# A hybrid decoder layer: the sums of the second head's attention weights on GpSimd

## The chip, the cores and the metric

One core of a Trainium2 chip runs the whole kernel. The metric is device time in microseconds, lower is better. Engines are named as the profile names them: PE is TensorE (PEld its weight loads), DVE is VectorE, ACT is ScalarE, POOL is GpSimd, SP is SyncE, which issues the DMAs.

## The reference

One layer over 2048 frames and 16 learned meta tokens, width 1024. A normalised input goes through one combined projection; its columns feed three mixers: forgetting attention (8 heads of 64), gated linear attention, and a gated linear recurrence. Their gated outputs go through an output projection, a second norm and the residual addition. What matters here is the forgetting attention:

```python
s = jnp.einsum('bhqd,bhkd->bhqk', qi, kf) * scale + cqi[..., None] - c[:, :, None, :]
mask = (kpos[None, :] <= qpos[:, None]) & valid[None, :]
p = jax.nn.softmax(jnp.where(mask, s, NEG), axis=-1)
return jnp.einsum('bhqk,bhkd->bhqd', p, vf)
```

The softmax needs, for each query, the sum of its weights over all keys. It is that sum which the change moves.

## The kernel before, in words

`hybrid_kernel` makes a list of jobs, each with a part that prepares (projections) and a part that mixes. While job i mixes, job i + 1 prepares: `merge` takes turns between the two in a fixed ratio, so the order of the instructions on each engine is fixed by the program. Jobs come in this order: the gated linear attention, the recurrence, then the 16 attention jobs, for each pair of heads p (0 to 3) and each chunk c of 512 queries (0 to 3). After them comes the output projection. A third stream, `wout_ready`, runs beside the attention jobs: it scales the output weights and splits them into halves (L1476 on DVE takes the remainder of a half, L1409 differences of blocks).

`fox_attend` (L1276) does one attention job with its two heads h = 0 and 1. It goes over 4c + 5 blocks of keys, j = 0, 1, and so on; a block has 128 keys, the last one 16. For each block:

- PE makes the logits of both heads in one pair of PSUM banks (`sq`, L1297, and on the diagonal a mask, L1303). From j = 4c on, `off` leaves out the queries that lie before the block, so that the width of a head is 512 at j = 4c, then 400, 272, 144 and, with 16 keys, 16.
- ACT takes the exponential of both heads into `pt` (L1305). There are three `pt` buffers, so the exponential of j + 3 needs everything that reads the `pt` of j to be done.
- The weights are added up over blocks in `za[0]` and `za[1]`, one for each head, with a row for each key of a block and a column for each query. At j = 1 DVE adds blocks 0 and 1 (L1310). From j = 2 on line 1313 adds block j to `za[h]`. Head 0 is always added on DVE. Head 1 is added on POOL at even j and on DVE at odd j.
- PE multiplies `pt` by the values (`fv`, L1325), two blocks behind.

At the end ACT copies the result (L1331), POOL multiplies it by the gate (L1332), and PE adds up the rows of `za` with a matrix of ones (L1336). The sums then go through DRAM to be spread and inverted. The rest of that is left for the next attention as two late functions: behind its add of j = 1 DVE takes the reciprocal, and behind its add of j = 2 POOL multiplies the result by it (L1351), for which it waits for the DMA of `rz`.

Beside the blocks of an attention runs `fox_prepare` of the next: projections (L485, L497), and for each 128 queries and each chunk of keys a product `mq` (L1231, L1235) whose maximum DVE takes straight from PSUM (`mj`, L1239). `mq` has one pair of banks, so the next product waits until DVE has read the last.

The framework puts in the waits: an engine runs its instructions in program order, and each waits for the writers and readers of its tiles.

Of the kernel before, what the change touches and what calls it, by code (L numbers as in the profile page):

```python
# [28 lines left out]
NCH = SEQ // CH  # L29
# [71 lines left out]
def unit(k, tag, shape, dt=F32, name=None):  # L101
    wide = tag in ("AT", "QA", "QB", "KA", "KB", "WC", "OO", "OX", "T", "Z", "ZZ", "WH", "WL")
    n = 1
    for d in shape[1:]:
        n *= d
    full = k.wk.tile([P, 2 * CH if wide else CH], dt, name=name or tag, tag=tag, bufs=BUFS[tag])
    ap = full[0:shape[0], 0:n]
    if len(shape) == 3:
        ap = ap.rearrange("p (a b) -> p a b", b=shape[2])
    return ap  # L110
# [5 lines left out]
def bank(k, tag="pj"):  # L116

    return k.ps.tile([P, CH], F32, name=tag, bufs=PBUFS[tag])


def pair(k, tag):

    return k.ps.tile([P, 2, CH], F32, name=tag, bufs=1)
# [44 lines left out]
def hybrid_kernel(tc, xT, x, w_grp, w_fa, vecs, w_a2, w_r, w_i, w_out, post_g, masks, out, yD=None):  # L168
    nc = tc.nc
    with ExitStack() as es:  # L170
# [56 lines left out]
        for p in range(4):  # L227
            for c in range(NCH):
                load = fox_loads(p + 1) if p < 3 else {}
                jobs.append((load.get(c, []), fox_prepare(k, p, c), fox_attend(k, p, c), 4 * c + 5,  # L230
                             FILL[c] if (p, c) != (3, 3) else LAST_FILL))
# [269 lines left out]
def rows_spread(k, i, ps):  # L501

    nc = k.nc
    D = k.rowD[i]
    zs = unit(k, "ZS", [P, CH], name="zs")
    nc.scalar.copy(out=zs, in_=ps)
    for h in range(2):
        nc.sync.dma_start(out=D[0, h:h + 1, :], in_=zs[64 * h:64 * h + 1, :])
    zt = small(k, "zt", [P, 8], bufs=2)
    nc.sync.dma_start(out=zt, in_=D[0].rearrange("h (q e) -> (h q) e", e=8))  # L510
    return D, zt


def rows_back(k, D, zt):
    k.nc.sync.dma_start(out=D[1].rearrange("h (q e) -> (h q) e", e=8), in_=zt)
# [754 lines left out]
def end_late(k):  # L1270
    for f in k.late:
        f(nullcontext())
    k.late = []


def fox_attend(k, p, c):  # L1276
    nc, st = k.nc, k.st
    qh, ql, qx = st.pop(("q", p, c))
    gate = st.pop(("gate", p, c))
    K = st["k", p]  # L1280
    pv = bank(k, "fv")
    za = [unit(k, "ZA", [P, CH], name="za") for _ in range(2)]
    nj = 4 * c + 5
    todo = []
    for j in range(nj):

        V = K.V[j // 4]
        d = j - 4 * c
        off = 0 if d <= 0 else P * d - NM
        m = NM if d == 4 else P  # L1290
        kk = slice(P * (j % 4), P * (j % 4) + m)
        sp = pair(k, "sq")
        pt = k.wk.tile([P, 2, CH], F32, name="pt", tag="PT", bufs=3)
        for i, (a, b) in enumerate(((K.hi, qh), (K.hi, ql), (K.lo, qh), (K.x, qx))):
            for h in range(2):
                hs = slice(64 * h, 64 * h + 64)
                nc.tensor.matmul(out=sp[0:m, h, off:], lhsT=a[j // 4][hs, kk], rhs=b[hs, off:], start=i == 0,  # L1297
                                 stop=i == 3 and d < 0)
        if d >= 0:
            v0 = NM if d == 0 else 0  # L1300
            v1 = NM if d == 4 else P
            for h in range(2):
                nc.tensor.matmul(out=sp[0:m, h, off:off + v1 - v0], lhsT=k.identb[0:m, 0:m],  # L1303
                                 rhs=k.trib[0:m, v0:v1], start=False, stop=True)
        k.exp = nc.scalar.activation(pt[0:m, :, off:], sp[0:m, :, off:], AF.Exp, scale=K.esc[0:m]).ins  # L1305
        for h in range(2):
            if j == 1:
                if off:
                    nc.vector.tensor_copy(za[h][:, 0:off], p0[:, h, 0:off])
                add = nc.vector.tensor_tensor(za[h][:, off:], p0[:, h, off:], pt[:, h, off:], op=ALU.add).ins  # L1310
            elif j > 1:
                eng = nc.gpsimd if h == 1 and j % 2 == 0 else nc.vector
                add = eng.tensor_tensor(out=za[h][0:m, off:], in0=za[h][0:m, off:], in1=pt[0:m, h, off:],  # L1313
                                        op=ALU.add).ins

        if 1 <= j <= 2 and k.late:
            k.late.pop(0)(k.tc.issue_after(add))
        if j == 0:
            p0 = pt
        todo.append((j, m, off, pt, V))  # L1320
        if len(todo) == 3 or j == nj - 1:
            for j1, m1, off1, pt1, V1 in todo[:1] if j < nj - 1 else todo:
                for h in range(2):
                    hs = slice(64 * h, 64 * h + 64)
                    nc.tensor.matmul(out=pv[hs, off1:], lhsT=V1[0:m1, j1 % 4, hs], rhs=pt1[0:m1, h, off1:],  # L1325
                                     start=j1 == 0, stop=j1 == nj - 1)
            todo = todo[1:]
        yield

    o = unit(k, "R", [P, CH], name="fo")  # L1330
    nc.scalar.copy(out=o, in_=pv)  # L1331
    nc.gpsimd.tensor_tensor(o, o, gate, op=ALU.mult)  # L1332
    zp = bank(k, "fx")
    for h in range(2):
        hs = slice(64 * h, 64 * h + 64)
        nc.tensor.matmul(out=zp[hs, :], lhsT=k.ones[:, 0:64], rhs=za[h], start=True, stop=True)  # L1336
    D, zt = rows_spread(k, NCH * p + c, zp)
    inv = k.w["fg", p][3]

    def rows(behind):  # L1340
        with behind:
            nc.vector.reciprocal(zt, zt)
        nc.vector.tensor_scalar(out=zt, in0=zt, scalar1=inv, scalar2=None, op0=ALU.mult)
        rows_back(k, D, zt)

    def scaled(behind):
        rz = unit(k, "RS", [P, CH], name="rz")
        for h in range(2):
            nc.sync.dma_start(out=rz[64 * h:64 * h + 64, :], in_=D[1, h:h + 1, :].to_broadcast([64, CH]))
        with behind:  # L1350
            nc.gpsimd.tensor_tensor(o, o, rz, op=ALU.mult)  # L1351
        k.store = k.mark = nc.sync.dma_start(out=k.yD[P * p:P * p + P, CH * c:CH * c + CH], in_=o).ins

    k.late = [rows, scaled]
    if (p, c) == (3, NCH - 1):
        end_late(k)
# [318 lines left out]
```

## Time and profile before

| | |
|---|---|
| median of 3 runs | 1989.29 us (1987.2 to 1992.66) |
| the profiled execution | 1977.47 us |
| its span, first to last instruction | 1975.8 us |
| PE busy | 1880.4 us (95%) |
| DVE busy | 1268.3 us (64%) |
| ACT busy | 1012.7 us (51%) |
| POOL busy | 565.4 us (29%) |
| adds of line 1313 on DVE | 208 |
| adds of line 1313 on POOL | 80 |

The profile is of one execution; its span is the time from the first to the last instruction. An engine is busy while it runs an instruction; waiting and issuing DMAs are not counted. The attention jobs lie between about 900 and 1676 us. In a timeline row the bracket at the end gives the idle time of the engine before the instruction and what ended it.

### The profile page before, as it was taken

The page shows a single profiled execution, that of the slowest core. Times are in us where ns is not written, and L with a number is a line of the kernel's source. Part 1 is how long each engine was busy: PE and PEld are TensorE (multiplying, and loading weights), DVE is VectorE, ACT ScalarE, POOL GpSimd, SP SyncE. Part 2 cuts the span into 40 slices and gives each one's busy share as a digit, 9 for nine tenths or more (in the row PEclk, how much of TensorE's full clock was granted, in tenths as well). Part 3 has the DMA queues.
Part 4 walks back from the last instruction along what each step waited for, and adds up shares of the span by engine and source line. Part 5 has one row for each costly group of instructions (what it writes and reads, how often), then busy time and mean ns, then how long its engine had stood idle before and what let it go on. Part 6 is the DMA issues. An engine that isn't in the chain of part 4 may idle for free. (4 is left out here: it accounts for less than half of the span.)

```text
span 1975.8 us, 39430 instructions
## 1 busy us (share of the span) xinstructions
PE 1880.4 (95%) x15988; PEld 976.2 (49%) x15988; DVE 1268.3 (64%) x2850; ACT 1012.7 (51%) x1561; POOL 565.4 (29%) x548
## 2 busy tenths in 40 slices
PE   6888999999999999999999999999999987999997
PEld 5555666666555555555434443444344422444443
DVE  6766454454787788673665368747874665667674
ACT  7755642344888887762345234523442335444441
POOL 3443133221434333320122111211221124433422
PEclk9999999999999999999999999999999988999999
DMA  6200121211211100121132113412431128723411
GB/s 225 76 8 29 43 86 29 75 55 30 82 52 45 44 22 22 43 74 44 61 101 69 30 46 118 128 45 65 118 97 44 44 59 294 234 87 122 134 43 64
DMA packets 116135, 152.69 MB, mean 77 GB/s; under 512 B 18793, under 2 KB 75817, under 8 KB 115953
## 3 DMA queue, kind: packets, MB, share of 16 engines
q1 hardware_dynamic: 115952, 150.18, 24.0%
q8 instruction: 125, 2.05, 0.4%
q14 instruction: 58, 0.47, 0.1%
HBM read 108.71 MB, written 41.33 MB: 76 GB/s over the span
## 5 line engine op out<-in xcount | busy, mean ns | idle before, releaser
L485 PE MATMUL pj<-xhl,whl 128*128 128x512 f16 (+3 forms) x3960 | 813.1, 356 | 16.1 <-ACT whl L437 7.4
L485 PEld LDWEIGHTS <-whl 128*128 128x128 f16 x3984 | 364.8, 98 | 405.1 <-issue 80.7
L1305 ACT ACTIVATE pt<-sq,consts 128x1024 f32<-128x1024 f32 (+4 forms) x176 | 163.4, 929 | 252.5 <-PE sq L1303 97.7
L1313 POOL TENSOR_TENSOR za<-za,pt 128x512 f32<-128x512 f32 (+1 forms) x80 | 99.0, 1238 | 535.4 <-ACT pt L1305 489.1
L1239 DVE CUSTOM_DVE_ANT_0 mj<-mq,CB 128x512 bf16<-128x512 f32 (+4 forms) x344 | 189.9, 579 | 56.7 <-PE mq L1231 28.5
L1604 PEld LDWEIGHTS <-whl 128*128 128x128 f16 x1344 | 130.6, 98 | 160.6 <-issue 4.4
L497 PEld LDWEIGHTS <-xhl 128*128 128x128 f16 (+1 forms) x3264 | 184.9, 97 | 31.6 <-issue 27.3
L497 PE MATMUL pj<-whl,xhl 128*128 128x128 f16 (+1 forms) x3024 | 189.6, 219 | 0.0
L1313 DVE TENSOR_TENSOR za<-za,pt 128x512 f32<-128x512 f32 (+3 forms) x208 | 121.3, 606 | 84.6 <-ACT pt L1305 81.2
L1325 PE MATMUL fv<-pt,fv 128*64 128x512 f32 (+4 forms) x688 | 171.3, 538 | 0.0
L1604 PE MATMUL pj<-xhl,whl 128*128 128x512 f16 x768 | 168.6, 380 | 0.0
L1297 PE MATMUL sq<-QA,KA 64*128 64x512 f16 (+4 forms) x1032 | 127.0, 341 | 9.5 <-ACT pt L1305 9.5
L1604 PE MATMUL pj<-ts,whl 128*128 128x512 f16 x576 | 125.7, 379 | 0.0
L563 DVE SCALAR_TENSOR_TENSOR xc<-lx,consts,xc 128x448 f32<-128x448 f32 (+1 forms) x120 | 93.4, 778 | 3.6
L1588 POOL TENSOR_TENSOR o<-o,xt 128x512 f32<-128x512 f32 x31 | 51.6, 1684 | 120.3 <-issue 91.7
L1570 ACT ACTIVATE sqo<-o 128x512 bf16<-128x512 f32 x32 | 20.1, 630 | 127.7 <-DVE o L1564 127.7
L521 ACT ACTIVATE gate<-pj,consts 128x512 f32<-128x512 f32 (+2 forms) x72 | 46.1, 641 | 72.4 <-PE pj L485 59.4
L1297 PEld LDWEIGHTS <-KA 64*128 64x128 f16 (+1 forms) x1032 | 40.3, 94 | 82.5 <-issue 59.9
L1610 DVE SCALAR_TENSOR_TENSOR o<-pj,consts,o 128x512 f32<-128x512 f32 x56 | 41.1, 745 | 61.1 <-PE pj L1604 56.9
L598 POOL TENSOR_TENSOR v<-a 128x448 f32<-128x448 f32 (+1 forms) x40 | 38.4, 961 | 129.5 <-ACT a L596 115.4
L1231 PE MATMUL mq<-KA,QA 64*128 64x512 f16 (+4 forms) x344 | 60.8, 342 | 10.6 <-DVE consts L1239 9.0
L522 DVE SCALAR_TENSOR_TENSOR gate<-gate,pj 128x512 f32<-128x512 f32 (+2 forms) x72 | 45.1, 627 | 39.4 <-ACT gate L521 38.1
(263 smaller groups left out, 2786.4 us busy)
## 6 DMA issues: line engine op xcount, KB each, us to landing
wr<-in_w_out_dram SPq DMA_DIRECT2D x64, 256.0 KB
y<-yD SPq DMA_DIRECT2D x32, 512.0 KB
raw<-in_w_grp_dram SPq DMA_DIRECT2D x28, 512.0 KB
wD<-ws SPq DMA_DIRECT2D x56, 256.0 KB
CB<-c32D SPq DMA_DIRECT2D x32, 256.0 KB
rawf<-in_w_grp_dram SPq DMA_DIRECT2D x16, 512.0 KB
xhl<-wD SPq DMA_DIRECT2D x16, 512.0 KB
xt<-in_x_dram SPq DMA_DIRECT2D x16, 512.0 KB
```

The lines of the kernel that those rows point to most:

```text
L485: nc.tensor.matmul(out=ps, lhsT=a[:, kt, 0:m], rhs=b[:, kt, u0:u0 + n], start=i == 0, stop=i == 23)
L497: nc.tensor.matmul(out=ps, lhsT=a[:, kt, u0:u0 + m], rhs=b[:, kt, :], start=i == 0, stop=i == 23)
L521: k.act = nc.scalar.activation(out, ps, AF.Tanh, scale=hinv).ins
L563: nc.vector.scalar_tensor_tensor(out=xc, in0=lx[:, j:j + n], scalar=cw(j), in1=xc, op0=ALU.mult, op1=ALU.add)
L1231: nc.tensor.matmul(out=ps[h][:, 0:n], lhsT=qh[hs, P * i:P * i + P], rhs=d.hi[pc][hs, 0:n], start=True, stop=pc < c)
L1239: nc.vector.tensor_tensor_reduce(out=junk[:, h, 0:n], in0=ps[h][:, 0:n], in1=d.cb[pc][:, h, 0:n], scale=1.0, scalar=-3e38, op0=ALU.add, op ...
L1297: nc.tensor.matmul(out=sp[0:m, h, off:], lhsT=a[j // 4][hs, kk], rhs=b[hs, off:], start=i == 0, stop=i == 3 and d < 0)
L1305: k.exp = nc.scalar.activation(pt[0:m, :, off:], sp[0:m, :, off:], AF.Exp, scale=K.esc[0:m]).ins
L1313: add = eng.tensor_tensor(out=za[h][0:m, off:], in0=za[h][0:m, off:], in1=pt[0:m, h, off:], op=ALU.add).ins
L1325: nc.tensor.matmul(out=pv[hs, off1:], lhsT=V1[0:m1, j1 % 4, hs], rhs=pt1[0:m1, h, off1:], start=j1 == 0, stop=j1 == nj - 1)
L1588: eng.tensor_tensor(out=o, in0=o, in1=xt[:, h, :], op=ALU.add)
L1604: nc.tensor.matmul(out=ps, lhsT=a[:, kt, :], rhs=w[b + kt // 4][:, :, kt % 4, :], start=kt + j == 0, stop=(kt, j) == (KT - 1, 2))
```

## The change

One line of `fox_attend` chooses the engine of the adds from j = 2 on. Before, POOL has the even blocks of head 1. After, POOL has all blocks of head 1 from j = 2 on, except in the last attention (p = 3, c = 3), where it has the even ones as before. Head 0 stays on DVE.

```diff
             elif j > 1:
-                eng = nc.gpsimd if h == 1 and j % 2 == 0 else nc.vector
+                eng = nc.gpsimd if h == 1 and (j % 2 == 0 or (p, c) != (3, NCH - 1)) else nc.vector
                 add = eng.tensor_tensor(out=za[h][0:m, off:], in0=za[h][0:m, off:], in1=pt[0:m, h, off:],
                                         op=ALU.add).ins
```

## Rows read from the trace of the kernel before

**Rows 1.** The page, part 1: busy time of each engine.

```profile
PE 1880.4 (95%) x15988; PEld 976.2 (49%) x15988; DVE 1268.3 (64%) x2850; ACT 1012.7 (51%) x1561; POOL 565.4 (29%) x548
```

**Rows 2.** The chain that ended last: start us, us, what.

```profile
1655.85 0.02 issue
...
1678.24 18.06 PE pj L1604 x81
```

**Rows 3.** Windows: busy time by stretch.

```profile
core 0: us, PE busy (x) PEld busy (x) DVE busy (x) ACT busy (x) POOL busy (x), PEclk, DMA share, GB/s
900.00:1600.00 700.00, 682.29 (x5111) 292.02 (x5109) 447.63 (x1264) 275.99 (x410) 129.08 (x105) 1.00 0.23 71
1180.00:1220.00 40.00, 38.18 (x246) 12.57 (x245) 36.23 (x89) 18.89 (x24) 8.96 (x8) 1.00 0.37 120
1380.00:1420.00 40.00, 37.52 (x234) 11.85 (x232) 35.81 (x87) 18.61 (x23) 10.08 (x8) 1.00 0.34 97
1425.00:1435.00 10.00, 8.51 (x45) 3.58 (x43) 5.93 (x27) 5.10 (x7) 0.00 (x0) 0.92 0.31 87
1435.00:1445.00 10.00, 10.00 (x54) 2.42 (x53) 9.11 (x16) 4.82 (x6) 1.34 (x1) 0.91 0.50 140
```

**Rows 4.** Waits of PE from 900 to 1600 us: total, times, longest.

```profile
PE mq L1231 <- DVE consts L1239: 8.3, 12, 1.5
PE sq L1297 <- ACT pt L1305: 3.5, 5, 2.0
```

**Rows 5.** Groups of DVE by form, 900 to 1680 us: busy us, mean ns, idle before.

```profile
L1313 DVE TENSOR_TENSOR za<-za,pt 128x512 f32<-128x512 f32 x120 | 85.1, 732 | 47.3 <-ACT pt L1305 44.1 <-POOL za L1313 2.8
...
L1476 DVE SCALAR_TENSOR_TENSOR ws<-wt,consts,ws 128x512 f16<-128x512 f32 x32 | 29.6, 926 | 6.6 <-ACT ws L1475 6.6
...
L1313 DVE TENSOR_TENSOR za<-za,pt 128x400 f32<-128x400 f32 x24 | 15.1, 658 | 10.2 <-ACT pt L1305 10.2
...
L1313 DVE TENSOR_TENSOR za<-za,pt 128x144 f32<-128x144 f32 x32 | 9.6, 336 | 16.7 <-ACT pt L1305 16.7
```

**Rows 6.** Groups of POOL by form, 900 to 1680 us.

```profile
L1313 POOL TENSOR_TENSOR za<-za,pt 128x512 f32<-128x512 f32 x48 | 79.3, 1653 | 344.6 <-ACT pt L1305 327.3 <-DVE za L1313 9.9 <-DVE consts L1239 4.6
...
L1313 POOL TENSOR_TENSOR za<-za,pt 128x272 f32<-128x272 f32 x16 | 15.9, 994 | 133.7 <-ACT pt L1305 121.0 <-DVE consts L1239 11.6 <-DVE za L1313 1.1
```

**Rows 7.** Timeline of p 1, c 3: start us, us, engine, instruction, idle before.

```profile
1274.17 0.69 DVE L1313 TENSOR_TENSOR za<-za,pt 128x512 f32<-128x512 f32 x1 [0.36 <-ACT pt L1305]
...
1274.22 1.77 POOL L1313 TENSOR_TENSOR za<-za,pt 128x512 f32<-128x512 f32 x1 [5.55 <-ACT pt L1305]
...
1274.79 1.76 DVE L1476 SCALAR_TENSOR_TENSOR ws<-wr,consts,ws 128x512 f16<-128x512 f32 x1
```

**Rows 8.** Timeline of p 2, c 2, j 7: two adds, then PE's wait.

```profile
1402.02 0.74 DVE L1476 SCALAR_TENSOR_TENSOR ws<-wr,consts,ws 128x512 f16<-128x512 f32 x1
...
1403.40 1.28 DVE L1313 TENSOR_TENSOR za<-za,pt 128x512 f32<-128x512 f32 x2
...
1404.83 1.27 POOL L1313 TENSOR_TENSOR za<-za,pt 128x512 f32<-128x512 f32 x1 [4.49 <-DVE za L1313]
...
1405.96 0.39 PE L1231 MATMUL mq<-KA,QA 64*128 64x512 f16 x2 [1.50 <-DVE consts L1239]
```

**Rows 9.** Timeline of p 3, c 2, j 2 and 3: L1476 beside POOL's add.

```profile
1587.53 1.16 DVE L1476 SCALAR_TENSOR_TENSOR ws<-wt,consts,ws 128x512 f16<-128x512 f32 x1
...
1589.35 0.39 PE L1231 MATMUL mq<-KA,QA 64*128 64x512 f16 x2 [0.97 <-DVE consts L1239]
```

**Rows 10.** Waits of POOL from 900 to 1600 us.

```profile
POOL fo L1351 <- DMA rz<-rowD: 26.1, 11, 4.6
```

**Rows 11.** Timeline of p 0, c 2: exponentials of j 3 and 6, and L1351.

```profile
995.42 1.11 ACT L1305 ACTIVATE pt<-sq,consts 128x1024 f32<-128x1024 f32 x1 [1.19 <-PE sq L1297]
...
998.25 1.27 POOL L1351 TENSOR_TENSOR fo<-fo,rz 128x512 f32<-128x512 f32 x1 [2.16 <-DMA rz<-rowD]
...
1002.86 1.11 ACT L1305 ACTIVATE pt<-sq,consts 128x1024 f32<-128x1024 f32 x1 [1.26 <-PE sq L1297]
```

## The prediction

> **What bounds the kernel now.** I read the busy shares first, then the chain that ended last, then the stretches in which the change lies. TensorE (PE) is busy 1880.4 us of 1975.8, VectorE (DVE) 1268.3 [rows 1]. The chain that ended last goes back only to 1655.85, into the last attention (p 3, c 3), which the change leaves alone; from 1678.24 it is the output projection [rows 2]. So the chain says nothing about the changed part, and I read that part by windows: from 900 to 1600 us PE is busy 682.29 of 700 us, DVE 447.63, GpSimd (POOL) 129.08 [rows 3]. PE has 17.7 us idle there, and no DVE relief can give back more. Of it, 8.3 us in 12 waits is PE standing in front of the next maximum product (`mq`, L1231) until DVE has read the last one (`mj`, L1239); 3.5 us is PE waiting for an exponential [rows 4]. DVE is nearly full only in the attentions with c 2: 36.23 of 40 us and 35.81 of 40 us in two of them [rows 3]. So DVE is a local bound, PE the general one.
>
> **What is moved.** An attention has 4c+5 steps. The adds of head 1 at odd j from 3 on number 2c+1: 16 per p, 64 in all, less 7 of the last attention: 57. By width: 31 of 512, 11 of 400 (j = 4c+1), 15 of 144 (j = 4c+3). Nothing else moves; j = 1 (L1310) and j = 2 stay, so the two late functions tied to those adds are issued where they were. POOL and DVE issue no DMA here, and SP's order is the same.
>
> **What DVE loses.** By the mean rows: 31 x 0.732 + 11 x 0.658 + 15 x 0.336 = 22.7 + 7.2 + 5.0 = 34.9 us [rows 5]. That is DVE time, not path: beside it PE computes. On the path lie only the waits of [rows 4].
>
> **What POOL gains, alone.** A 512 add holds POOL 1.27 us when nothing is in its way [rows 8]; the means of 1.653 and 0.994 (272 wide) [rows 6] have waiting in them. Taking 1.27 and, by width, estimates of 0.99 for 400 and 0.36 for 144: 39.4 + 10.9 + 5.4 = 56 us. POOL has 571 us idle in the stretch, so it has room.
>
> **What the two do to each other.** At 1274.17 DVE adds for 0.69 us; POOL's add, started 0.05 later, takes 1.77; the DVE subtraction behind (L1476) takes 1.76 instead of 0.74 [rows 7, 8]. So the two take turns: POOL waits for DVE's add, then DVE's next instruction with two SBUF operands waits for POOL's. The maxima, which read PSUM, show no such loss. The means of L1476 carry it (926 against 740) [rows 5]. The Trainium skill (SBUF — State Buffer, Who interferes with whom) goes further: the loser stands still for the whole of the winner's instruction. By that rule each moved add would lengthen the taking of turns by 1.27 - 0.69 us, and that is rival C, which I work out below from rows.
>
> **What PE sees of it.** Seven of the 12 waits are of 0.5 us or more. Four have the pair of adds of an odd j ahead of the maxima in DVE's queue, as at 1403.40: two adds take 1.28 us, the maxima wait behind them, and PE stands 1.50 us [rows 8]. Without the second add each shrinks by up to 0.69: 0.5 + 0.65 + 0.69 + 0.69 = 2.5 us won. The other three, of 0.97 (at 1589.35), 0.97 and 1.28 us, come behind a DVE instruction that POOL held up: L1476 took 1.16 us at 1587.53 beside the add of j = 2 [rows 9]. The change does nothing for these and makes more of them: 3.2 us over the 111 POOL two-operand instructions there (80 adds, 31 on `fo`) is 0.029 us each; 57 more give 1.6 us. For this unseen price the near end is 0 (no such wait behind a moved add) and the far end is the 9.4 us of rival C; I take 1.6 because it is the same instruction in the same stage. Sum: 2.5 - 1.6 = 0.9 us won.
>
> **The waits that change hands.** Now `za[1]` goes from engine to engine at every step; afterwards it stays on POOL from j = 2 on, and DVE no longer stands behind POOL in its own queue. But odd adds now queue behind the multiplication by `rz` (L1351), which waits for a DMA: 26.1 us in 11 waits, at most 4.6 [rows 10]. Worked through in one attention of c 2: L1351 runs 998.25 to 999.52 [rows 11]; the add of j = 3, ready since 996.53, would run until 1000.8, those of j = 4 and 5 until 2.1 and 3.4 us past 1000. Exponential 6 needs the buffer of j = 3 and starts at 1002.86 [rows 11], so 2 us are left. Even at 4.6 us of waiting, one step is late by about 2 us, and it catches up, since steps take 2.3 us or more and an add 1.78 at most. Cost: 0, hidden by the three `pt` buffers; without that cover about 2 us per attention. At an attention's end the 144-wide add comes before the 16-wide one on POOL, and the sum product (L1336) is several us behind: 0.
>
> **Forecast, A.** 1977.47 us (the profiled execution; span 1975.8 and 1.7 around it) less 0.9 is 1976.6. The median of the runs is 11.8 us above that execution, so I carry the difference over: **1988.4 us**. About 6 us (0.3%) is what a measurement of this kernel can tell from no change.
>
> **Rival B, faster.** DVE is the bound in the c 2 attentions, and all 8.3 us of waits for the maxima go, since 35 us of DVE relief is four times as much. The clock may add to it: it is 0.92 and 0.91 in two 10 us windows after PE stood idle around 1430 [rows 3], 1.7 us of work lost. Together 10 us: 1979.3. For it: 36 of 40 us busy. Against it: three of the seven large waits are POOL's own doing. It decides if the waits for L1239 fall under 2.5 us.
>
> **Rival C, slower.** Taking turns costs more than the move gives. Place: the four c 2 attentions, 20 moved adds (12 of 512, 4 of 400, 4 of 144). Where the next DVE instruction has two SBUF operands, it starts 1.27 after the first add instead of 0.69: 12 x 0.58 and, by width, 4 x 0.45 + 4 x 0.16, together 9.4 us, if all of it reaches PE: 1998.7. For it: L1476 at 1.76. Against it: often a maximum follows, which isn't held up, and DVE has slack for c 1 and 3. It decides from the point where about two thirds of that delay reach PE (6 us). The Trainium skill (Perfetto Trace Analysis, Optimizing Scalar/DVE Operations) says that offloading between GpSimd and DVE might not help; that would be A or C, and the trace so far shows the mechanism, not its size.
>
> **Rival D, slower.** POOL falls behind in several attentions and the exponential waits for `pt`: 2 us in each of the 4 with c 2, 8 us: 1997. Against it: the 2 us left above.
>
> **Chances.** A 0.60, B 0.22, C 0.14, D 0.04. That gives faster 0.22, the same 0.60, slower 0.18. The range reaches from B to just past D: 1980 to 1997; A alone would be 1983 to 1994.
>
> **What would show it.** DVE L1313 at 151 instructions instead of 208, POOL at 137 instead of 80; DVE busy 20 to 35 us less; L1476's mean above 926. A is right if PE's idle time from 900 to 1600 stays between 12 and 23 us. It is wrong if PE's waits for L1239 nearly vanish (B) or pass 14 us (C), or if exponentials wait for POOL's `za` by more than 2 us at a time with PE idle behind (D). The steps that could fail are the 0.029 us per POOL instruction, taken from three waits only, and the assumption that PE's order hides DVE's new place.

## The result, and the profile after

The kernel after takes 1997.32 us (median of 8 runs, 1993.3 to 2003.43), the kernel before 1988.09 us beside it (8 runs). The ratio is 1.0052, with a 95% interval of 1.0033 to 1.0072: the change costs about 9 us, where the prediction forecast no measurable difference and a range that ends at 1997.0.

The profiled execution of after took 1996.98 us, with a span of 1995.3. Its page, busy time by engine, stands against [rows 1]:

```profile
PE 1881.8 (94%) x15988; PEld 981.3 (49%) x15988; DVE 1259.9 (63%) x2793; ACT 1011.9 (51%) x1561; POOL 637.0 (32%) x605
...
L1313 POOL TENSOR_TENSOR za<-za,pt 128x512 f32<-128x512 f32 (+3 forms) x137 | 174.2, 1272 | 494.7 <-ACT pt L1305 481.1
...
L1313 DVE TENSOR_TENSOR za<-za,pt 128x512 f32<-128x512 f32 (+3 forms) x151 | 99.6, 663 | 88.7 <-ACT pt L1305 85.8
```

The 57 adds have moved as said: 151 on DVE, 137 on POOL. But DVE is only 8.4 us less busy and POOL 71.6 us more, against 34.9 and 56 in the prediction's sums. The window from 900 to 1600 us and PE's waits in it, against [rows 3, 4]:

```profile
900.00:1600.00 700.00, 671.51 (x5054) 291.69 (x5051) 429.21 (x1173) 268.75 (x404) 190.01 (x153) 1.00 0.24 71
```

```profile
PE mq L1231 <- DVE consts L1239: 12.0, 16, 2.5
PE sq L1297 <- ACT pt L1305: 6.6, 7, 2.8
PE pj L485 <- DVE gate L522: 2.2, 3, 1.2
PE sq L1297 <- DVE consts L1239: 1.5, 2, 0.9
```

PE has 28.5 us idle instead of 17.7. Its waits for the maxima went from 8.3 to 12.0 us, and its waits for exponentials from 3.5 to 6.6. What DVE lost in adds it got back in part as longer instructions; the DVE groups by form from 900 to 1680 us, and POOL's, against [rows 5, 6]:

```profile
L1313 DVE TENSOR_TENSOR za<-za,pt 128x512 f32<-128x512 f32 x88 | 73.2, 836 | 48.6 <-ACT pt L1305 46.0 <-POOL za L1313 2.4
L1476 DVE SCALAR_TENSOR_TENSOR ws<-wt,consts,ws 128x512 f16<-128x512 f32 x32 | 33.1, 1035 | 6.6 <-ACT ws L1475 6.2 <-issue 0.3
```

```profile
L1313 POOL TENSOR_TENSOR za<-za,pt 128x512 f32<-128x512 f32 x78 | 130.3, 1671 | 315.3 <-ACT pt L1305 311.7 <-DVE za L1313 3.0 <-POOL fo L1351 0.2
```

The longest wait for a maximum shows what stands in a row. The timeline of p 2, c 2 in the kernel after:

```profile
1406.29 1.27 POOL L1313 TENSOR_TENSOR za<-za,pt 128x512 f32<-128x512 f32 x1 [0.59 <-ACT pt L1305]
...
1406.78 1.32 DVE L1409 TENSOR_TENSOR wt<-wr,wt 128x512 f32<-128x512 f32 x1
...
1408.33 1.51 POOL L1351 TENSOR_TENSOR fo<-fo,rz 128x512 f32<-128x512 f32 x1 [0.77 <-DMA rz<-rowD]
...
1408.63 1.75 DVE L1476 SCALAR_TENSOR_TENSOR ws<-wr,consts,ws 128x512 f16<-128x512 f32 x1
...
1409.80 1.71 POOL L1313 TENSOR_TENSOR za<-za,pt 128x512 f32<-128x512 f32 x1
...
1410.31 0.68 DVE L1239 CUSTOM_DVE_ANT_0 mj<-mq,CB 128x512 bf16<-128x512 f32 x1
...
1411.66 0.39 PE L1231 MATMUL mq<-KA,QA 64*128 64x512 f16 x2 [2.48 <-DVE consts L1239]
```

Two pieces of the output weights are held up beside POOL's work: L1409 beside the add of j = 3, a moved one (1.32 us, 0.68 where nothing is in its way), and L1476 beside L1351, the multiplication by `rz` (1.75 us, 0.74 in [rows 8]). The maxima stand behind them, and PE stands 2.48 us in front of the next maximum product. L1351 is not a moved instruction; the kernel before runs it too. So this wait is only in part the price of a moved add.

The two profiled executions differ by 19.5 us, the medians by 9.2. Of the 19.5, 8.9 us lie ahead of the first exponential (at 898.5 before, at 907.4 after), in stages that the change doesn't touch; in all the profiles below this first exponential lies between 899.3 and 911.4 us, whatever was changed behind it. So from here on I compare lengths of the attention stage only: from the first exponential of an attention to that of the next, added up over p, up to the first exponential of p 3, c 3. Worked out so from the starts of L1305, in us (the last column is the length of the stage times what its mean granted clock lacks to 1):

```
                                          p 0    p 1    p 2    p 3    sum   PE idle in it  clock
before                                   197.1  198.4  198.6  131.7  725.7  23.3                5.0
after                                    196.2  203.2  204.8  132.8  737.0  35.6                2.9
e1  before, order held                   197.0  198.0  197.7  131.6  724.3  24.3                2.4
e2  adds moved, order of before          196.3  200.2  203.2  131.8  731.5  28.4                5.2
e3  adds not moved, order of after       197.0  205.1  202.0  132.8  736.9  31.9                6.8
e4  adds left out, order of before       197.0  199.3  199.0  132.8  728.0  26.1                4.6
e5  e1 and maxima first                  197.1  199.6  198.5  131.1  726.3  25.6                1.8
e6  e2 and maxima first                  196.3  199.8  200.0  130.7  726.8  25.9                2.1
e7  POOL fills, order of before          196.4  200.0  199.6  132.2  728.2  27.3                2.7
e8  POOL reads too, order of before      203.0  202.9  205.6  137.6  749.2  40.7               10.5
e9  after and maxima first               196.2  204.2  206.3  131.7  738.4  34.6                5.1
e10 e3 and maxima first                  197.0  203.8  201.7  131.3  733.8  31.0                4.4
e11 p 0 and p 3 moved, order of before   196.2  198.6  197.8  131.7  724.3  24.0                2.3
e12 p 1 and p 2 moved, order of before   197.4  201.8  203.4  130.5  733.0  31.3                3.8
e13 e1 with PE of p 1, c 2 as in after   197.0  204.1  197.7  131.6  730.3  28.3                3.9
e14 after, projections between           198.8  202.3  212.8  132.3  746.2  35.1               12.0
e15 e1, projections between              199.1  201.5  201.5  130.9  732.9  27.5                7.4
e16 e6, projections between              198.5  203.0  200.2  129.8  731.6  26.5                6.6
```

After p 3, c 3 begins, all of them take 350.5 to 353.4 us more. Each length is of one execution; before and e1, which have one order, differ by 1.4 us. The loss of after lies in p 1 and p 2, where 72 of the 88 pieces of the output weights (L1476, L1409) run on DVE; p 0, which has none, gains 0.9 us.

In every row the sum less the last two columns is 697.3 to 699.1 us. So whatever a version costs in this stage is time in which PE stands idle, or time in which it works at the lower of its two granted clocks (0.50, that is 1.2 GHz of 2.4). Where such a fall is shown below, it begins in one of PE's waits or just behind it.

### The profile page after: what moved, and what is told of

It reads as the page before. It is cut to its first block, busy times and chain, and to the rows that moved or that the text cites. A ratio compares the mean times of both kernels' runs of the same rounds, so it can differ in the third digit from the quotient of the medians.

```text
span 1995.3 us, 39524 instructions
## 1 busy us (share of the span) xinstructions
PE 1881.8 (94%) x15988; PEld 981.3 (49%) x15988; DVE 1259.9 (63%) x2793; ACT 1011.9 (51%) x1561; POOL 637.0 (32%) x605
## 5 line engine op out<-in xcount | busy, mean ns | idle before, releaser
L485 PE MATMUL pj<-xhl,whl 128*128 128x512 f16 (+3 forms) x3960 | 810.8, 356 | 21.3 <-ACT whl L437 5.7
L485 PEld LDWEIGHTS <-whl 128*128 128x128 f16 x3984 | 365.5, 98 | 407.3 <-issue 78.8
L1313 POOL TENSOR_TENSOR za<-za,pt 128x512 f32<-128x512 f32 (+3 forms) x137 | 174.2, 1272 | 494.7 <-ACT pt L1305 481.1
L1305 ACT ACTIVATE pt<-sq,consts 128x1024 f32<-128x1024 f32 (+4 forms) x176 | 163.4, 928 | 266.7 <-PE sq L1303 99.4
L1239 DVE CUSTOM_DVE_ANT_0 mj<-mq,CB 128x512 bf16<-128x512 f32 (+4 forms) x344 | 189.8, 579 | 65.6 <-PE mq L1231 32.9
L1313 DVE TENSOR_TENSOR za<-za,pt 128x512 f32<-128x512 f32 (+3 forms) x151 | 99.6, 663 | 88.7 <-ACT pt L1305 85.8
```

The lines of the kernel that those rows point to most:

```text
L485: nc.tensor.matmul(out=ps, lhsT=a[:, kt, 0:m], rhs=b[:, kt, u0:u0 + n], start=i == 0, stop=i == 23)
L1239: nc.vector.tensor_tensor_reduce(out=junk[:, h, 0:n], in0=ps[h][:, 0:n], in1=d.cb[pc][:, h, 0:n], scale=1.0, scalar=-3e38, op0=ALU.add, op ...
```

## The experiments

**The order is not fixed by the program text.** The description ahead of the prediction says that the order on each engine is fixed by the program. That is false. The framework re-orders instructions when it compiles, and when 57 adds change engine it arrives at another order for everything: comparing the orders of the two built programs from the attention jobs on, without the moved adds, 688 of PE's 6258 instructions stand at another place, 146 of DVE's 1186, 37 of SP's, 24 of ACT's and 4 of POOL's. For example, in p 2, c 2 DVE has in before a piece (L1476), a maximum (L1239), a piece (L1409), another maximum and a piece again (L1476); in after the two maxima come ahead of all three. So two theories stood against each other: M, the move itself costs, because POOL and DVE take turns; and O, the new order costs. To part them, the experiments hold the order: between each two consecutive instructions of an engine, from the attention jobs on, a dependency without a semaphore is put in, from a list taken from a built program.

```diff
+def pin(tc, nc):
...
+        for x, y in zip(seq, seq[1:]):
+            tc.add_manual_dep(traced[y], traced[x].name, mybir.DependencyInfo(
+                mybir.DependencyClass.NoSync, mybir.DependencyReason.DATA), reason="order")
...
         hybrid_kernel(tc, *args)
+        pin(tc, nc)
```

### e1 to e4: the move and the order, each alone

e1 is the kernel before with its order held, and a control.

> The kernel before, with the order of every engine's instructions from the attention jobs on written down and held to what the compile-time scheduler had chosen. A control for the next two: the program is the same but for where tiles lie. All theories: within 4 us of the kernel before (ratio 0.998 to 1.002), PE idle from 900 to 1600 us 14 to 21 us. If it is off by more, where tiles lie matters by itself.

Measured: 1985.63 us, ratio 0.9993 (0.998 to 1.0005). Holding the order costs nothing that can be measured.

e2 is the kernel after (the line of the change) with the order of before; the moved adds stand on POOL where after has them.

> The 57 adds on GpSimd, but PE, ACT, DVE and SP held to the order of the kernel before. Theory M (the move itself: GpSimd's adds hold up DVE's two-operand instructions, and PE waits for DVE): slower than before by 7 to 12 us, nearly all of the change's 9.2 us. Theory O (the scheduler saw the adds on GpSimd, chose another order for PE, DVE and ACT, and that order is worse): between 3 us faster and 2 us slower than before, as the prediction's sum had it.

Measured: 1994.1 us, 1.0049 (1.003 to 1.0068). The attention that loses most is p 2, c 1 (51.3 us instead of 48.1 in e1). There a moved add, that of j = 3, holds up L1409, and PE waits behind it. In e1 (last line) POOL has no add at that place, and PE no wait. (The wait in e2 stands at `sq`, which needs no maximum; more on that below.)

```profile
1353.95 1.72 POOL L1313 TENSOR_TENSOR za<-za,pt 128x512 f32<-128x512 f32 x1
...
1354.68 1.53 DVE L1409 TENSOR_TENSOR wt<-wr 128x512 f32<-128x512 f32 x1
...
1356.49 0.82 PE L1297 MATMUL sq<-QA,KA 64*128 64x512 f16 x6 [1.39 <-DVE consts L1239]
```

```profile
1357.92 0.68 DVE L1409 TENSOR_TENSOR wt<-wr 128x512 f32<-128x512 f32 x1
```

e3 is the kernel before (no add moved) with the order of after.

> The adds on the engines of before, but PE, ACT, DVE and SP held to the order of the changed kernel. Theory M: within 3 us of before. Theory O: slower than before by 6 to 12 us.

Measured: 1994.61 us, 1.0047 (1.0032 to 1.0061).

e4 leaves the 57 adds out, in the order of before:

```diff
-            elif j > 1:
+            elif j > 1 and not (h == 1 and j % 2 and (p, c) != (3, NCH - 1)):
```

> The 57 adds are left out altogether (the sums of head 1 lack the odd blocks, but for the last attention), order of before held. This is the relief of DVE alone, without GpSimd's part: the prediction's term of 2.5 us, at most 10. All theories: 1 to 8 us faster than before. If it is no faster, DVE's relief was worth nothing, and the prediction's gain term falls.

Measured: 1987.68 us, 1.0015 (1.0 to 1.003). PE's waits from 905 to 1640 us, in e1, e2 and e4:

```profile
PE mq L1231 <- DVE consts L1239: 8.9, 12, 1.5
...
PE sq L1297 <- ACT pt L1305: 3.5, 6, 1.6
```

```profile
PE mq L1231 <- DVE consts L1239: 7.9, 13, 1.3
PE sq L1297 <- ACT pt L1305: 4.2, 6, 1.3
PE sq L1297 <- DVE consts L1239: 4.0, 3, 1.9
```

```profile
PE mq L1231 <- DVE consts L1239: 7.4, 11, 1.3
PE sq L1297 <- ACT pt L1305: 5.1, 8, 2.3
...
PE sq L1297 <- DVE consts L1239: 1.7, 3, 1.0
```

Each theory is right in the run where it forecast a loss, about 9 us in both, and wrong in the run where it forecast none. The two losses don't add up: with the order of after the move costs next to nothing more (1.0052 against 1.0047). And taking 57 adds away from DVE altogether wins nothing: PE's waits at `mq` are 1.5 us less than in e1, those for exponentials and maxima at `sq` 3.3 us more. That the ones turned into the others is not shown: for exponentials alone the kernel before waits 6.1 us in this window and e1 3.5, with one order.

### e5 and e6: maxima ahead of the pieces

In DVE's order each piece that stands directly ahead of a maximum changes places with it, 64 times; all else as in e1 (e5) or e2 (e6).

```diff
 DVE, for example in p 2, c 2
-L1409 wt
 L1239 mj
+L1409 wt
```

> The kernel before with its order held, but in DVE's order 64 pieces of the output weights (L1476, L1409), each of which stood directly ahead of a maximum (L1239), change places with that maximum; no other engine's order changes. Theory O (what the new order costs is that the pieces stand ahead of the maxima): it comes out faster than the kernel before by 4 to 9 us, ratio 0.9955 to 0.998, and PE's waits for L1239 between 905 and 1640 us fall from 8.9 us to under 6. Rival M (DVE's order counts for nothing, only the taking of turns does): ratio within 0.9985 to 1.0015 and the waits within 2 us of 8.9.

Measured: 1987.89 us, 1.0012 (1.0001 to 1.0023). The waits for L1239 at `mq` fall to 6.1 us, but there are 2.4 us of them at `sq`, and the time doesn't fall: Theory O, put in this way, is wrong, and the rival has the time right and the waits at `mq` not quite.

> The adds on POOL as in the kernel after, the order of before held on the other engines, with the 64 exchanges of e5 in DVE's order. Theory M (the move costs about 7 us by the taking of turns, since DVE's next instruction with two SBUF operands waits for POOL): e2 stood at 1.0049, and the piece that POOL holds up now stands behind the maximum, so half or more of the 7 us goes: ratio 0.999 to 1.002. If what the move costs has nothing to do with which DVE instruction stands behind the adds, it stays at 1.004 to 1.006.

Measured: 1985.37 us, 1.0003 (0.999 to 1.0016). The cost of the move is gone, though L1476 still takes 0.96 and 1.01 us in the mean. So in the order of before what the move costs hangs on which DVE instructions stand between POOL's add and a maximum that PE waits for.

### e7 and e8: is it POOL's reading?

e7: instead of the moved add POOL copies 8 numbers of `pt`, fills a scratch tile twice and copies 8 numbers again. e8: the adds stay on DVE, and POOL does one of the same width into a scratch tile.

```diff
+            elif j > 1 and h == 1 and j % 2 and (p, c) != (3, NCH - 1):
...
+                nc.gpsimd.tensor_copy(zd[0:1, 0:8], pt[0:1, h, off:off + 8])
+                for i in range(2):
+                    nc.gpsimd.memset(zd[:, 0:CH - off], 0.0)
+                add = nc.gpsimd.tensor_copy(zd[0:1, 0:8], pt[0:1, h, off:off + 8]).ins
```

```diff
+                if h == 1 and j % 2 and (p, c) != (3, NCH - 1):
...
+                    nc.gpsimd.tensor_tensor(out=zd[0:m, off:], in0=pt[0:m, h, off:], in1=gate[0:m, off:], op=ALU.add)
```

> The 57 adds are left out (those blocks are missing from the sums), and in their place POOL fills a scratch tile with zeros (two fills of half the time each) between two copies of 8 numbers of pt, so that POOL is as long busy and lets go of pt as late, but reads next to nothing of SBUF. The order of before is held. Theory M by turn taking: without POOL's reads nothing holds DVE up, so it comes out as e4 (1.0015), 1.0 to 1.003, stage 726 to 729 us, and L1476 keeps the mean it has in e4. Rival L (it is POOL's lateness with pt and with its own queue that costs, not the reads): as e2, 1.004 to 1.006, stage 731 us or more.

Measured: 1989.31 us, 1.003 (1.0017 to 1.0043), stage 728.2 us. L1476 keeps its 0.93 us. The ratio lies at the top of M's range, and the interval reaches into L's and overlaps that of e2: the run doesn't part the two theories cleanly.

> The 57 adds stay on DVE, and POOL does for each an add of the same width into a scratch tile, reading pt and the gate. The order of before is held. Nothing is computed differently. Theory M by turn taking: POOL's reads hold DVE up as in e2 while DVE has not been relieved, so slower than e2: 1.005 to 1.009. Rival L: POOL's queue is as long as in e2, pt is let go as late, and DVE's load hardly matters (e4): 1.004 to 1.006. If neither holds, 1.000 to 1.002.

Measured: 2007.71 us, 1.0124 (1.0107 to 1.0142), worse than either theory asked. DVE's group of 512-wide adds and PE's wait in e8:

```profile
L1316 DVE TENSOR_TENSOR za<-za,pt 128x512 f32<-128x512 f32 x104 | 108.0, 1061 | 21.6 <-ACT pt L1305 21.2
```

```profile
PE mq L1231 <- DVE consts L1239: 21.2, 24, 2.9
```

(The waits are those from 905 to 1640 us; in e1 they are 8.9 us.) In e1 these adds take 0.729 us. So a POOL add beside DVE, with DVE's own load unchanged, costs 0.43 us for each of the 57 (24.6 us in all). What is held up here is not the pieces (L1476 takes 0.875 and 0.795 us in the mean, less than the 0.926 and 0.928 of e1) but DVE's own adds, 104 of them by 0.332 us. In e2 73 adds in the same window lose 0.141 us each (0.870 against 0.729). So the move's price is of the same kind, but how much of e8's it pays is not shown.

### e9 and e10: the same exchange in the order of after

As e6 and e5, but in the order of after (55 exchanges): e9 with the adds moved, e10 without.

> The kernel after with its own order, but in DVE's order the 55 pieces of the output weights (L1476, L1409) that stand directly ahead of a maximum (L1239) change places with it. Theory P (whatever the order, the loss is a piece that POOL holds up, ahead of a maximum that PE waits for): the kernel after stands 9 to 11 us above the one before; half or more of that goes, ratio 0.999 to 1.0025, PE's waits for L1239 between 905 and 1640 us under 9 us instead of 14.1. Rival Q (the new order costs in another place, PE's own sequence): 1.004 to 1.006.

Measured: 1997.46 us, 1.0068 (1.0042 to 1.0094), waits for L1239 13.1 us.

> The adds on the engines of the kernel before, the new order held as in e3 (which stood at 1.0047), with the 55 exchanges in DVE's order. Theory P: in e3, too, pieces stand ahead of maxima and POOL's even adds hold some of them up; ratio 0.999 to 1.0025. Rival Q: PE's and ACT's new sequence is what costs, and the exchanges change nothing, as in e5, where they brought nothing in the old order: 1.004 to 1.006.

Measured: 1996.55 us, 1.0045 (1.0025 to 1.0065). P falls. Q stands, though e9 lies above its range and only the interval reaches into it: in the order of after the loss isn't in the places of the pieces.

### e11 and e12: where the move costs

```diff
-                eng = nc.gpsimd if h == 1 and j % 2 == 0 else nc.vector
+                eng = nc.gpsimd if h == 1 and (j % 2 == 0 or (p in (0, 3) and (p, c) != (3, NCH - 1))) else nc.vector
```

and `or p in (1, 2)` for e12, both with the order of before.

> Only the 25 adds of p 0 and p 3 move to POOL, the order of before held. The pieces of the output weights run on DVE from p 1, c 2 on, most of them in p 1 and p 2. Theory M (the move costs by a piece held up ahead of a maximum): p 0 gains 0.7 us as in e2, p 3 stays within 1 us: ratio 0.9985 to 1.0005, stage 722 to 725 us. If the cost of the move were spread over all moved adds (0.16 us each, 9 us over 57): 4 us slower, 1.002.

Measured: 1986.18 us, 0.9997 (0.9979 to 1.0016), stage 724.3 us.

> Only the 32 adds of p 1 and p 2 move to POOL, the order of before held; the complement of e11. Theory M: all the loss of e2 (1.0049) is here: 1.004 to 1.006, p 1 and p 2 each 2 to 6 us longer than in e1. If the cost were spread over all moved adds: 5 us slower, 1.0025.

Measured: 1993.14 us, 1.004 (1.0021 to 1.0058), stage 733.0 us. The cost of the move is not spread over the adds; it lies in p 1 and p 2, where most pieces run. (The 16 pieces of p 3 cost nothing in e11.)

### e13 to e16: what in the order of after costs

PE's sequences differ most in the attentions p 1, c 2 and p 2, c 2. There 6 and 7 groups of maximum products in the order of after follow the group before them with no projection (L485) between, 4 and 3 in that of before. e13 takes PE's sequence of after in p 1, c 2 alone; e14 (in the order of after, with the move), e15 (as e1) and e16 (as e6) bring projections forward in PE's sequence of all four c 2, so that at least two stand in each such gap.

```diff
 PE, e13, p 1, c 2
 L1297 sq
-L485 pj
 L1231 mq
...
+L485 pj
```

```diff
 PE, e14 to e16, c 2
 L1231 mq
 L1297 sq
+L485 pj
+L485 pj
 L1231 mq
...
-L485 pj
-L485 pj
```

> The kernel before with its order held on every engine but PE, and on PE only in the attention p 1, c 2, which has there the sequence of the kernel after (six of its groups of maximum products, instead of four, follow the group before with no projection between). The adds stay where they were. Theory Q (the new order's cost is PE's sequence in the c 2 attentions): p 1, c 2 takes 52.5 us or more instead of 50.3 (e3: 54.1), and the attentions of p 0, p 2 and p 3 stay as in e1; the whole time 1.001 to 1.003. Rival S (it takes DVE's new sequence as well, or ACT's): p 1, c 2 within 0.8 us of 50.3, ratio 0.999 to 1.001.

Measured: 1990.44 us, 1.0019 (1.0005 to 1.0032). p 1, c 2 takes 56.3 us instead of 50.3, every other attention is within 0.1 us of e1. Q holds: one attention's PE sequence costs 6.0 us there, with no add moved and DVE's order untouched (4.0 us more idle time than in e1, the rest mostly the clock). The same place in e1 and in e13, by the timeline; e1 first:

```profile
1207.44 1.93 PE L1325 MATMUL fv<-pt,fv 128*64 128x512 f32 x6
...
1209.31 0.60 PE L485 MATMUL pj<-xhl,whl 128*128 128x512 f16 x2
...
1209.38 1.23 DVE L1409 TENSOR_TENSOR wt<-wr 128x512 f32<-128x512 f32 x1
...
1209.84 0.60 PE L1297 MATMUL sq<-QA,KA 64*128 64x512 f16 x3
...
1210.07 0.59 PE L1231 MATMUL mq<-KA,QA 64*128 64x512 f16 x2
```

```profile
1210.59 1.08 PE L1325 MATMUL fv<-pt,fv 128*64 128x512 f32 x4
...
1211.60 0.39 PE L1231 MATMUL mq<-KA,QA 64*128 64x512 f16 x2
...
1212.54 1.23 DVE L1409 TENSOR_TENSOR wt<-wr 128x512 f32<-128x512 f32 x1
1213.69 0.68 DVE L1239 CUSTOM_DVE_ANT_0 mj<-mq,CB 128x512 bf16<-128x512 f32 x1
...
1214.43 1.46 PE L1297 MATMUL sq<-QA,KA 64*128 64x512 f16 x6 [2.44 <-DVE consts L1239]
```

DVE does the same in both, the L1409 beside POOL's add included. In e1 PE has values and projections to work on meanwhile; in e13 it comes to its next wait for a maximum at once and stands 2.44 us. And it comes out of the wait at half clock, as the windows of e13 show (the clock is the third number from the end):

```profile
1205.00:1212.00 7.00, 6.68 (x40) 1.70 (x37) 6.34 (x16) 4.38 (x6) 2.75 (x3) 1.00 0.48 147
1212.00:1214.40 2.40, 0.00 (x0) 0.00 (x0) 2.40 (x7) 0.48 (x1) 1.22 (x1) 0.94 0.99 289
1214.40:1216.00 1.60, 1.57 (x8) 0.47 (x7) 1.60 (x3) 0.00 (x0) 0.00 (x0) 0.50 0.64 232
1216.00:1218.00 2.00, 2.00 (x8) 0.39 (x6) 1.30 (x5) 1.11 (x1) 0.00 (x0) 0.62 0.41 135
```

0.50 is 1.2 GHz of 2.4: six `sq` take 1.46 us instead of 0.82, and by the clock 1.6 us of work are lost until it is back (1.6 x 0.50 + 2.0 x 0.38). This isn't the rule for every wait: the one of 2.48 us in after, shown above, left the clock at 1.00.

Two things limit this reading. The wait stands at `sq`, which needs no maximum, and not at the `mq` behind it; so e13 parts PE's sequence from DVE's and from the move, but not from the places of waits that come with it (more on this at the wait of 1.94 us in e2, below). And in both timelines a row of `mq` (1210.07 in e1, 1211.60 in e13) starts before DVE has read the group before it (until 1211.21 and 1214.37), which the one pair of banks doesn't allow; so the names in PE's rows may be out by a group here. How long PE stood, and that DVE's maximum ended it, doesn't hang on that.

> The kernel after with its own order, but on PE, in the c 2 attentions, projections (L485) come forward so that at least two stand between one group of maximum products and the next (84 moves). Theory Q: with work between the maxima PE need not stand in front of them; half or more of the 9 to 11 us goes, 0.999 to 1.0025, PE's waits for L1239 between 905 and 1640 us under 9 us. Rival S: 1.004 to 1.007, waits for L1239 within 2 us of 14.1. If the projections themselves come too early (their weights or their bank not ready), slower than after, with PE waits at L485.

Measured: 2002.34 us, 1.0068 (1.0048 to 1.0088).

> The kernel before with its order held, but on PE, in the c 2 attentions, at least two projections between one group of maximum products and the next (78 moves). Theory Q: also here PE stands 8.9 us in front of maxima; 2 to 6 us of it go, 0.997 to 0.9992. If the projections come too early: 1.000 to 1.004.

Measured: 1993.13 us, 1.003 (1.0017 to 1.0043).

> The adds on POOL, the order of before, the 64 exchanges of e6 and the 78 moves of e15 together. e6 stood at 1.0003. If the two remedies add up: 0.996 to 0.9992, the version that beats both kernels. If PE has nothing left to win: 1.000 to 1.002.

Measured: 1994.05 us, 1.003 (1.0011 to 1.0048).

The remedy fails. More idle time is not the main reason: against the same version without this edit PE is idle 0.5 us less in e14 and only 0.6 us more in e16 (3.2 more in e15), but the clock takes 9.1, 4.5 and 5.0 us more. The timeline of PE in p 1, c 2 of e15 shows where such a fall begins. From 1190 to 1225 us PE is idle for 0.4 us (1.8 in e1, up to 1224). But the projections that were brought forward had stood between the last maximum products of the attention, and there PE waits now, where e1 has no wait but the last one:

```profile
1230.13 0.39 PE L1231 MATMUL mq<-KA,QA 64*128 64x512 f16 x2 [1.62 <-DVE consts L1239]
...
1231.94 0.61 PE L1231 MATMUL mq<-KA,QA 64*128 64x512 f16 x2 [0.89 <-DVE consts L1239]
...
1245.35 0.60 PE L485 MATMUL pj<-xhl,whl 128*128 128x512 f16 x2 [1.38 <-ACT whl L437]
```

The clock falls to 0.50 at 1231.7, inside the second of these waits. Projections are a fixed stock of work to wait with; in e15 they were spent early and missing at the end. Whether the same holds at every fall in e14 and e16 was not followed. No version here beats the kernel before beyond its interval; e1, e6 and e11 are level with it.

## Why the prediction was wrong

**The step that failed is "Nothing else moves", with "SP's order is the same"**, and the assumption under it, which the prediction named as one that could fail, that PE's order hides DVE's new place. PE's order did not stay. e3 shows that the new order alone costs 1.0047, and e13 that a single attention of PE's new sequence costs 6.0 us there. No rival had this mechanism. Rows of before couldn't show it, since they hold one order only. With the order held the move still costs 1.0049 (e2), and there two terms of the sum were wrong.

**The gain of 2.5 us** from shorter queues ahead of the maxima was mis-sized: with the adds gone altogether (e4) it is not there (1.0 to 1.003). The waits at `mq` do shrink, by 1.5 us, but those for exponentials and for maxima at `sq` are 1.6 and 1.7 us more. e4 also has waits at other places than e1 (see below), so a small gain may be hidden in it.

**The price of 0.029 us per POOL add** was too low. With the order of before the move costs 0.34% more than leaving the adds out (e2 less e4), 6.8 us or 0.12 us per add, and all of it in p 1 and p 2 (e11, e12). The prediction took it from three waits and spread it evenly over all POOL instructions.

**A second part of it is not turn taking.** The wait of 1.94 us in e2 at p 2, c 2, and the same place in e1 (first):

```profile
1402.69 1.75 DVE L1476 SCALAR_TENSOR_TENSOR ws<-wr,consts,ws 128x512 f16<-128x512 f32 x1
...
1403.75 0.82 PE L1297 MATMUL sq<-QA,KA 64*128 64x512 f16 x6
...
1404.97 0.68 DVE L1239 CUSTOM_DVE_ANT_0 mj<-mq,CB 128x512 bf16<-128x512 f32 x1
...
1405.73 0.39 PE L1231 MATMUL mq<-KA,QA 64*128 64x512 f16 x2
```

```profile
1402.71 1.75 DVE L1476 SCALAR_TENSOR_TENSOR ws<-wr,consts,ws 128x512 f16<-128x512 f32 x1
...
1405.00 0.68 DVE L1239 CUSTOM_DVE_ANT_0 mj<-mq,CB 128x512 bf16<-128x512 f32 x1
...
1405.74 1.02 PE L1297 MATMUL sq<-QA,KA 64*128 64x512 f16 x6 [1.94 <-DVE consts L1239]
```

DVE runs at the same times, within 0.03 us (in both L1476 is held up by L1351 and not by a moved add: POOL runs it from 1402.13 and 1402.15 on, for 1.77 us). What differs is the instruction that carries the wait. In the built program of e1 this `sq` waits for ACT, and the `mq` behind it for DVE; in e2 the `sq` waits for DVE, and the `mq` for PE. So in e2 PE stops for the maximum one group of logits earlier than it has need of it, and works behind it at a granted clock of 0.71 (1405.7 to 1407 us) and then 0.50 (1407 to 1409). Why the framework places the wait otherwise once the add has left DVE was only read in the programs and not tried. e4 and e7 have the same places of waits, so some of their 0.15 and 0.3% may be this. e6 has such waits too (3.9 us in 5 at `sq` for L1239), and its 1.0003 shows that they cost little once the maxima come early.

**Rival C** had the mechanism of e2 in part (a DVE instruction held up, and PE behind it), and its 9.4 us are near the 9.7 that e2 lost (0.0049 of 1988). Its place was too narrow: p 2, c 1 is 3.2 us longer in e2 than in e1 and p 1, c 3 1.6 us, not the c 2 alone; that its time lies near the measured one is in part luck. Its marker, waits for L1239 over 14 us, did not come: 12.0, and 13.5 with those at `sq`.

**Rival D's** marker did not come. In after exponentials do wait 24.3 us for POOL's `za`, 15 times from 900 to 1600 us, against 9.1 us in 6 waits in before. But only one is longer than 2 us (2.25 at 1480.00; before has one of 2.25 at 1460.88), and PE isn't idle for more than 0.3 us at a time in the 6 us from there. Nor is it the cause: e6 has 28.2 us of such waits, 18 times, and costs nothing.

**What was right:** the counts of 151 and 137, L1476's mean above 926 (1035), POOL's room, and the multiplication by `rz` at L1351, whose waits for the DMA shrank to 19.6 us against [rows 10]. DVE's relief was short of 20 to 35 us over the whole kernel, since the remaining 512-wide adds lost 0.104 us each (88 of the 89 lie in the window: 9.2 us) and the pieces lost another 9.1 us. The Trainium skill (SBUF — State Buffer, Who interferes with whom) says that the loser stands still for the winner's instruction; L1476 at 1.75 us against 0.74 agrees: in after it ends 0.54 us behind the L1351 beside it. e8 shows what standing still is worth when nothing is given back for it.

**What stays open:** why the losses of the move and of the order don't add up in the kernel after, what PE's new sequence in p 2 alone costs (p 2 is 4.3 us longer in e3 than in e1; only p 1, c 2 was tried), and what DVE's new sequence alone would do with PE's old one. Why the clock falls after some waits and not after others stays open too; even before and e1, with one order, lose 5.0 and 2.4 us to it.

## What to carry to other kernels

Under a framework that schedules, moving an instruction to another engine changes the order and the places of waits on all of them: compare the built orders first, and part "the move" from "the order" by holding the order, before any wait is explained. Relief of an engine with slack is worth something only where the bound engine waits for it; a run like e4, in which the work is simply left out, asks that directly. Add up the idle time of the bound engine and what its granted clock lacks: here the two together are nearly the whole loss. And before GpSimd gets two-operand work beside VectorE, look at which VectorE instruction comes next, and whether the bound engine waits behind it.

## What was not expected of the hardware

An add on POOL whose result nothing reads (e8) costs 0.43 us of the whole time for each, about a third of the 1.27 us that it takes alone, and does so in p 0 too (203.0 against 197.0 us), where no piece runs. POOL fills of like length (two of 0.533 us, between two copies of 8 numbers, in e7) cost DVE's 512-wide adds little: 0.820 us against 0.789 with nothing in their place (e4) and 1.061 beside POOL's adds (e8). And TensorE worked for more than 3 us at a granted clock of 0.50 after waits of 2.44 and 1.94 us (e13, e2) and at 1.00 after one of 2.48 us (after, at 1411.66), so that a wait can cost nearly twice what the list of waits says.
